# Attention stage of a hybrid decoder trunk: order of the K loads, the class copies, the 1/z chain and the V weights

## The chip, the cores and the metric

The kernel runs on one core of a Trainium2 chip. Its metric is the device time of one launch in microseconds (us), the median of several runs. Beside the times there is one profiled execution, whose trace holds every instruction. The engines are TensorE (PE in the profile; its weight loads are PEld), VectorE (DVE), ScalarE (ACT), GpSimd (POOL) and SyncE (SP). Each takes its instructions in the order in which the program was written for it. SyncE issues most loads, POOL issues the stores and some loads.

## The reference

Two layers over 1024 positions of width 1024, in float32: a gated short convolution with a SwiGLU, then dilated attention with a SwiGLU. The change lies in the attention, whose core is this:

```python
BRANCHES = ((128, 1), (512, 4), (2048, 16))      # window, dilation; 16 heads of 64
qkv = (h @ w_qkv).reshape(bsz, seq, 3, N_HEADS, HEAD_DIM)
for window, dilation in BRANCHES:
    # query t attends to keys t - j*dilation, j = 0..window//dilation
    s = q.k * HEAD_DIM ** -0.5 + rel_bias[t5_bucket(dist)]
    lse = logsumexp(s); o = exp(s - lse) @ v
alpha = softmax(stack(lses))                      # over the three branches
o = sum(alpha * outs)
x = x + o.reshape(bsz, seq, D_MODEL) @ w_out
```

The softmax over branches joins the three to one: the exponentials of all branches share one maximum and one sum z per query and head, and the output is their weighted sum of V times 1/z.

## The kernel before

The program is an order written out by hand: Python generators are stepped in a fixed pattern, and what they emit goes to each engine's queue in that order. Every float32 operand of a large product is split into a high and a low part (`split`, L132): ScalarE rounds (L142), VectorE subtracts (L143), and TensorE makes three products of the parts. Operands live in `PAGES = 41` pages of 128 x 1024 (`page`); a new tile takes a page that an earlier one has left. PSUM has 8 banks, taken in turn.

Weights stand in a list, `raw_src`, in the order of their use. `ensure(upto)` makes all split weights up to an index, and for each it loads raw weights two further (`get_raw`, `load_raw`, L156 on SyncE). `take(key, ahead)` calls `ensure` for the next weight and `ahead` more, and hands the weight out; `op_state[1]` is the index of the next one to be taken. For the V groups a weight is a slab of 128 x 1024, two for each group.

**The attention stage** runs `slot(n)` for n = 0 to 16, called block n here; p, a = divmod(n, 2) is the pair of heads and the head in it. Up to block 13 (`LAG`) a block has two halves of eight steps:

- first half: the scores of head n (`scores`: matmuls L1556 and L1557, additions of the bias on VectorE L1567 to L1607, at the end the maximum over partitions on POOL, L1610), with steps of the dense work in between;
- second half: the values of head n-1 (`values`: L1629, at the end four copies of z and o from PSUM by ScalarE, L1652 and L1653), the softmax of head n at step i = 3 (subtractions L1618, exponentials L1619), the class copies of the next head's K (`classes`, L1540), and more dense work.

The dense work is one generator, `fill()`, 15 steps a block: value groups 1 and 2 (`value_tiles(g, j)`, 40 steps each: j is the half of the positions, b4 one of four tiles of five steps, L1501 to L1503, evicted by ScalarE L1506, stored by POOL L1510), the projections of Q and K for pairs 6 and 7 (36 steps each, `qk.emit` L1129 to L1138), value group 3, and the first half of the output product (`ao`, L370 to L372). Value group 0 runs ahead of block 0. Group 2 (V2 in what follows) starts in block 2, the projections in block 5, group 3 in block 10, the output product in block 12. In block 12 the attended tiles of pairs 0 to 3 are split too.

At the start of a block SyncE gets these loads, in this order: in odd blocks V of the pair (`load_values`, six transfers into `vx`, which has one buffer: they wait for the values of the pair before), then for head n+1 the bias tables (two transfers, L1452 and L1453, two buffers), K (two, L1530 and L1531), Q (two, L1533) and Q's low part (L1534).

**1/z.** In odd blocks `finish(p - 1)` runs for the pair before, in steps: z to DRAM (L1661, POOL) at i = 0 of the first half; z back with 128 partitions (`zc`, L1664, POOL) at i = 3; reciprocal on VectorE (L1666) and its store (`rdram`, L1667, POOL) at i = 0 of the second half; two loads of 1/z spread over 64 partitions each (L1670, POOL) at i = 4. `attended()` then multiplies o by 1/z (L1717, VectorE) and stores it (L1718, POOL), at i = 2 of the second half of the next, even block.

Of the kernel before, what the change touches and what calls it, by code (L numbers as in the profile page):

```python
# [45 lines left out]
SOFT = 4  # L46
FIN0 = 2
AO_WIDE = 5
AO = 4
LAG = 13  # L50
# [48 lines left out]
def trunk(ctx: ExitStack, tc: tile.TileContext, x, gains_in, cwi, ck, cwo, wqkv, wo, relb,  # L99
# [8 lines left out]
    def page(name, dt=F32):  # L108
        return pages.tile([128, 1024], dt, name=name, tag="page", bufs=PAGES)
# [6 lines left out]
    def bank():  # L116
        return psum.tile([128, 512], F32, name="bank", tag="bank")
# [31 lines left out]
    ops, made, op_state = [], {}, [0, 0]  # L149
# [13 lines left out]
    def ensure(upto):  # L163
        while op_state[0] < min(upto + 1, len(ops)):
            key = ops[op_state[0] + 1][0] if op_state[0] + 1 < len(ops) else None
            if key in sums_of:
                sums_of.pop(key)()
            made[op_state[0]] = ops[op_state[0]][1]()
            op_state[0] += 1

    def take(key, ahead=1):
        i = op_state[1]
        assert ops[i][0] == key, (ops[i][0], key)
        ensure(i + ahead)
        op_state[1] += 1
        return made.pop(i)
# [198 lines left out]
    def run(*gens):  # L375
        for _ in zip(*gens):
            pass
        for g in gens:
            for _ in g:
                pass  # L380
# [1068 lines left out]
    def load_bias(h):  # L1449
        t = scope["pool"].tile([128, L1 + L2], F32, name="bias", tag="bias", bufs=2)  # L1450
        base = tables.offset + h * G3
        nc.sync.dma_start(t[:, 0:L1], bass.AP(tensor=tables.tensor, offset=base, ap=[[1, 8], [A1, 16], [1, L1]]))  # L1452
        nc.sync.dma_start(t[:, L1:L1 + L2], bass.AP(tensor=tables.tensor, offset=base + G0,  # L1453
                                                    ap=[[1, 32], [A2, 4], [1, L2]]))
        return t
# [10 lines left out]
    def attention(norm, qk):  # L1466
        KS, KC, QS, wv = {}, {}, {}, []
# [22 lines left out]
        def value_tiles(g, j):  # L1490

            if j == 0:
                wv[:] = [take(("v", g, i), 1) for i in range(2)]
            v = page("v")
            for b4 in range(4):
                t = 4 * j + b4
                b = bank()[:, :256]
                for k in range(KT):
                    (hi, lo), (whi, wlo) = qk.h[j][k], wv[k // 4]
                    a, c = slice(b4 * 128, b4 * 128 + 128), slice(k % 4 * 256, k % 4 * 256 + 256)  # L1500
                    nc.tensor.matmul(b, hi[:, a], whi[:, c], start=k == 0, stop=False)  # L1501
                    nc.tensor.matmul(b, hi[:, a], wlo[:, c], start=False, stop=False)
                    nc.tensor.matmul(b, lo[:, a], whi[:, c], start=False, stop=k == KT - 1)  # L1503
                    if k % 2:
                        yield
                nc.scalar.activation(v[:, b4 * 256:b4 * 256 + 256], b, AF.Identity, scale=norm.r[:, t:t + 1])  # L1506
                yield
            vd = vdram[g]
            for r in range(4):
                nc.gpsimd.dma_start(bass.AP(vd.tensor, vd.offset + (512 * j + r) * 256,  # L1510
                                          [[16 * 256, 32], [4 * 256, 4], [1, 256]]), v[32 * r:32 * r + 32])

        def load_values(p):
            src = vdram[p // 2]
            for a in range(2):
                off = src.offset + p % 2 * 128 + a * 64
                dims = slice(128 * a, 128 * a + 64)
                nc.sync.dma_start(vx[:, 0:8, dims], bass.AP(src.tensor, off, [[256, 128], [128 * 256, 8], [1, 64]]))
                for h in range(2):
                    nc.sync.dma_start(vx[:, 8 + 4 * h:12 + 4 * h, dims],  # L1520
                                        bass.AP(src.tensor, off + 512 * 256 * h, [[1024, 128], [256, 4], [1, 64]]))

        def load_kq(n):

            p, a = divmod(n, 2)
            k, q = qk.kq[p, 1], qk.kq[p, 0]
            rows = lambda t, r: bass.AP(t.tensor, t.offset + r * S, [[S, 64], [1, S]])
            n0, n1 = (slice(64 * i, 64 * i + 64) for i in (a, 1 - a))
            KS[n], QS[n] = page("ka", F32R), page("qa", F32R)
            nc.sync.dma_start(KS[n][n0].bitcast(F32), rows(k, 64 * a))  # L1530
            nc.sync.dma_start(KS[n][n1].bitcast(F32), rows(k, 128 + 64 * a))  # L1531
            for m in (n0, n1):
                nc.sync.dma_start(QS[n][m].bitcast(F32), rows(q, 64 * a))  # L1533
            nc.sync.dma_start(qlo[a][n0].bitcast(F32), rows(q, 128 + 64 * a))  # L1534

        def classes(n):

            KC[n] = page("kca", F32R)
            for h in range(2):
                nc.scalar.activation(KC[n][:, half(h)], view(KS[n], h * HALF, [[1, 4], [4, 128]]), AF.Copy)  # L1540
                yield
# [171 lines left out]
        def attended():  # L1713

            while put_off:
                p, o, z = put_off.pop()
                nc.vector.tensor_tensor(out=o, in0=o, in1=z, op=ALU.mult)  # L1717
                nc.gpsimd.dma_start(odram[p], o)  # L1718

        put_off = []  # L1720
        OZ, acts = {}, {}

        def slot(n, dense, ndense, late=0, hook=iter(())):

            def other(k):
                for _ in range(k):
                    next(dense, None)

            p, a = divmod(n, 2)
            if n < H:  # L1730
                new = dict(bias=bias.pop(n))
                sc = scores(p, a, new)
            else:
                sc = iter(())
            if n <= LAG and n % 2:
                load_values(p)
            if n + 1 < H:
                bias[n + 1] = load_bias(n + 1)
                load_kq(n + 1)
            if n:  # L1740
                q, b = divmod(n - 1, 2)
                if b == 0:
                    OZ[q] = page("o"), page("z")
                old = live.pop(n - 1)
                old.update(o=OZ[q][0], z=OZ[q][1])
                pv = values(q, b, old)
            else:
                pv = iter(())
            extra = later = iter(())
            lagged = n <= LAG  # L1750
            if n + 1 < H:
                later = classes(n + 1)
            if lagged and a and p:
                extra = finish(p - 1)
            used = 0
            if lagged:
                for i in range(8):
                    next(sc, None)
                    if n or i % 2:
                        other(1)  # L1760
                        used += 1
                    if i in (0, 3):
                        next(extra, None)
                run(sc)
            else:
                if a == 0 and not late:
                    other(1)
                    used += 1
                for i in range(8):
                    next(sc, None)  # L1770
                    next(pv, None)
                    next(pv, None)
                    if i >= late and i % 2 == 0:
                        other(1)
                        used += 1
                run(sc)
                run(pv)
                if a == 0:
                    extra = finish(p - 1)
                if a == 0 and n < H:  # L1780
                    load_values(p)
            left = max(ndense - used, 0)
            for i in range(8):
                next(pv, None)
                next(pv, None)
                if i == 2:
                    attended()
                if i in (0, 4) if lagged else i < FIN0 or i > SOFT:
                    next(extra, None)
                if i in (0, 1):  # L1790
                    next(later, None)
                if i == (3 if lagged else SOFT):
                    if n < H:
                        live[n] = new
                        run(softmax(new))
                if i >= SOFT:
                    next(hook, None)
                other(left * (i + 1) // 8 - left * i // 8)
            run(pv)
            run(extra)  # L1800
# [56 lines left out]
        acts.update(split_attended(load_attended(range(AO, 7))))  # L1857
        ensure(ahead_ao)
        slot(H, dense, 15)
        run(dense)  # L1860
        return acts
# [199 lines left out]
```

## Time and profile before

| | us |
|---|---|
| runs: lowest, median, highest of 3 | 2145.25, 2153.15, 2157.45 |
| profiled execution, its own time | 2144.75 |
| its span, first to last instruction | 2142.9 |
| busy in the span: PE, DVE, ACT, POOL | 2109.1, 1747.6, 1008.1, 255.8 |
| mean granted TensorE clock | 0.994 |
| first and last maximum of the attention blocks begin at | 1122.7, 1428.6 |

A row of the timeline is start, duration, engine, line, operation and tiles; what stands in brackets is how long the engine was idle just before, and what ended that. A row of the waits is who waited for whom, the total in us, how often, and the longest. Tiles are named out<-in. Memory transfers are read by the line that issued them.

### The profile page before, as it was taken

To read this page: it belongs to the slowest core of one execution; us is meant where nothing else is said; L and a number is where in the kernel's file an instruction comes from. 1 tells how busy PE (TensorE), PEld (TensorE's weight loads), DVE (VectorE), ACT (ScalarE), POOL (GpSimd) and SP (SyncE) were. 2 spreads that over 40 slices of the span, in tenths; PEclk is the share of its full clock that TensorE was granted. 3 is DMA by queue.
4 is the path that set the end of the run, shared out by engine and by line. 5 is a ranking of instruction groups with operands and counts; after the bars stand their busy time and mean duration, and the time that the engine had idled before them with its cause. 6 is when DMAs were issued, how large, how long until landed. Compare 5 with 4: busy or idle time off the path is not lost. (4 is left out here: it accounts for less than half of the span.)

```text
span 2142.9 us, 30996 instructions
## 1 busy us (share of the span) xinstructions
PE 2109.1 (98%) x11086; PEld 1808.6 (84%) x11086; DVE 1747.6 (82%) x3272; ACT 1008.1 (47%) x1848; POOL 255.8 (12%) x370
## 2 busy tenths in 40 slices
PE   9999999999999999999999999899999999999998
PEld 7788878888888888877898989898788888888887
DVE  8898769988888888868956677787998888888876
ACT  7333426443434464336545545455543434456435
POOL 1000000111101000000322332321010101001000
PEclk9999999999999999999999999999999999999999
DMA  7322642333333576341766777765223333368432
GB/s 218 93 94 69 228 136 69 107 110 104 103 109 112 171 225 195 100 158 41 273 196 168 181 196 191 226 193 163 72 91 101 109 108 106 105 201 236 160 94 79
DMA packets 143353, 304.90 MB, mean 142 GB/s; under 512 B 48942, under 2 KB 55326, under 8 KB 143200
## 3 DMA queue, kind: packets, MB, share of 16 engines
q1 hardware_dynamic: 107488, 201.94, 31.6%
q0 software_dynamic: 28080, 86.29, 12.7%
q10 hardware_dynamic: 7632, 14.70, 1.8%
q8 instruction: 88, 1.44, 0.3%
q14 instruction: 65, 0.53, 0.1%
HBM read 212.48 MB, written 83.05 MB: 138 GB/s over the span
## 5 line engine op out<-in xcount | busy, mean ns | idle before, releaser
L563 PE MATMUL bank<-b,w 128*128 128x512 f32 x1952 | 760.8, 390 | 4.8 <-DVE w L143 4.6
L561 PE MATMUL bank<-b,w 128*128 128x512 f32 x1952 | 762.8, 391 | 2.1 <-ACT w L142 1.7
L562 PE MATMUL bank<-b,w 128*128 128x512 f32 x1952 | 760.4, 390 | 0.6 <-DVE b L872 0.6
L563 PEld LDWEIGHTS bank<-b,w 128*128 128x128 f32 x1952 | 366.4, 188 | 85.6 <-DVE w L143 9.5
L561 PEld LDWEIGHTS bank<-b,w 128*128 128x128 f32 x1952 | 366.7, 188 | 78.6 <-ACT w L142 2.8
L562 PEld LDWEIGHTS bank<-b,w 128*128 128x128 f32 x1952 | 366.7, 188 | 76.5 <-DVE b L872 1.2
L142 ACT ACTIVATE w<-combo 128x512 fp32r<-128x512 f32 (+2 forms) x488 | 249.1, 540 | 231.5 <-DVE combo L190 214.7
L143 DVE TENSOR_TENSOR w<-combo,w 128x512 fp32r<-128x512 f32 (+2 forms) x488 | 277.0, 581 | 37.7 <-ACT w L142 37.0
L567 ACT ACTIVATE part<-bank 128x512 f32<-128x512 f32 x186 | 110.7, 596 | 388.8 <-PE bank L563 387.1
L143 DVE TENSOR_TENSOR w<-raw,w 128x512 fp32r<-128x512 f32 (+2 forms) x342 | 190.0, 577 | 37.2 <-ACT w L142 37.2
L571 DVE TENSOR_TENSOR part<-part,bank 128x256 f32<-128x256 f32 (+1 forms) x366 | 171.1, 498 | 31.1 <-PE bank L563 16.6
L142 ACT ACTIVATE w<-raw 128x512 fp32r<-128x512 f32 (+2 forms) x342 | 166.7, 530 | 45.2 <-PE bank L563 12.2
L370 PE MATMUL bank<-w_hi,w 128*128 128x512 f32 (+1 forms) x400 | 153.3, 383 | 3.3 <-ACT w_hi L142 3.3
L371 PE MATMUL bank<-w_lo,w 128*128 128x512 f32 (+1 forms) x400 | 150.0, 375 | 0.7 <-DVE w_lo L143 0.7
L372 PE MATMUL bank<-w_hi,w 128*128 128x512 f32 (+1 forms) x400 | 149.8, 375 | 0.7 <-DVE w L143 0.7
L791 DVE TENSOR_TENSOR x<-x,bank 128x512 f32<-128x512 f32 x136 | 92.8, 682 | 29.1 <-PE bank L563 29.1
L492 DVE TENSOR_TENSOR x<-x,bank 128x512 f32<-128x512 f32 (+1 forms) x104 | 66.3, 643 | 55.7 <-PE bank L372 55.1
L190 DVE TENSOR_TENSOR combo<-raw 128x512 f32<-128x512 f32 (+1 forms) x172 | 111.4, 648 | 0.0
L370 PEld LDWEIGHTS bank<-w_hi,w 128*128 128x128 f32 x400 | 75.8, 189 | 16.5 <-ACT w_hi L142 3.5
L371 PEld LDWEIGHTS bank<-w_lo,w 128*128 128x128 f32 x400 | 75.8, 190 | 14.4 <-DVE w_lo L143 1.6
L372 PEld LDWEIGHTS bank<-w_hi,w 128*128 128x128 f32 x400 | 75.8, 189 | 14.5 <-DVE w L143 1.1
L554 DVE TENSOR_TENSOR b<-hin,b 128x512 fp32r<-128x512 f32 x126 | 79.6, 686 | 9.5 <-ACT b L553 9.5
(247 smaller groups left out, 3497.6 us busy)
## 6 DMA issues: line engine op xcount, KB each, us to landing
hin<-part SPq DMA_DIRECT2D x126, 256.0 KB
raw<-in_ffn_w_gate SPq DMA_DIRECT2D x44, 512.0 KB
raw<-in_ffn_w_up SPq DMA_DIRECT2D x44, 512.0 KB
part<-sum POOLq DMA_DIRECT2D x72, 256.0 KB, 2.3
raw<-in_ffn_w_down SPq DMA_DIRECT2D x48, 384.0 KB
raw<-in_attn_w_qkv SPq DMA_DIRECT2D x27, 512.0 KB
raw<-in_conv_w_in SPq DMA_DIRECT2D x24, 512.0 KB
part<-part POOLq DMA_DIRECT2D x36, 256.0 KB, 2.4
```

Of the source, the lines that this page charges most:

```text
L142: nc.scalar.activation(hi, src, AF.Copy)
L143: eng.tensor_tensor(out=lo, in0=src, in1=hi, op=ALU.subtract)
L190: eng.tensor_tensor(out=c, in0=a, in1=b, op=op)
L370: nc.tensor.matmul(b, whi[:, a], ahi[:, s], start=first, stop=False)
L371: nc.tensor.matmul(b, whi[:, a], alo[:, s], start=False, stop=False)
L372: nc.tensor.matmul(b, wlo[:, a], ahi[:, s], start=False, stop=last)
L561: nc.tensor.matmul(b, hi[:, a], bhi, start=start and k == 0, stop=False, skip_group_check=True)
L562: nc.tensor.matmul(b, hi[:, a], blo, start=False, stop=False, skip_group_check=True)
L563: nc.tensor.matmul(b, lo[:, a], bhi, start=False, stop=k == n - 1, skip_group_check=True)
L567: nc.scalar.activation(t, b, AF.Copy)
L571: nc.vector.tensor_tensor(out=t, in0=t, in1=b, op=ALU.add)
L791: nc.vector.tensor_tensor(out=X[n][:, half(h)], in0=X[n][:, half(h)], in1=b, op=ALU.add)
```

## The change

- In `value_tiles` the two slabs of a group are taken without asking for the next weight. In the second half of a group (j = 1), ahead of its second and third tile, the next weight and the one after it are asked for.
- In a block's loads K of the next head comes first. The V loads of an odd block come right behind that K, ahead of Q; the bias tables come last.
- The class copies are made at i = 1 and 2 of the second half instead of 0 and 1.
- `finish` of a pair: the z store and load stay; the reciprocal and its store move from i = 0 to i = 6 of the odd block's second half, the loads of the spread 1/z from i = 4 there to i = 2 of the next block's first half. `attended()` moves from i = 2 to i = 5 of the second half in blocks up to 14.

```diff
@@ value_tiles
             if j == 0:
-                wv[:] = [take(("v", g, i), 1) for i in range(2)]
+                wv[:] = [take(("v", g, i), 0) for i in range(2)]
             v = page("v")
             for b4 in range(4):
+                if j and b4 in (1, 2):
+                    ensure(op_state[1] + b4 - 1)
@@ load_kq
             nc.sync.dma_start(KS[n][n1].bitcast(F32), rows(k, 128 + 64 * a))
+            if n <= LAG + 1 and n % 2 == 0 and n:
+                load_values(p - 1)
             for m in (n0, n1):
@@ slot
-        put_off = []
+        put_off, ending = [], []
...
-            if n <= LAG and n % 2:
-                load_values(p)
             if n + 1 < H:
+                load_kq(n + 1)
                 bias[n + 1] = load_bias(n + 1)
-                load_kq(n + 1)
...
             if lagged and a and p:
-                extra = finish(p - 1)
+                ending.append(finish(p - 1))
...
-                    if i in (0, 3):
-                        next(extra, None)
+                    if a and ending and i in (0, 3):
+                        next(ending[-1])
+                    if a == 0 and ending and i == 2:
+                        run(ending.pop())
...
+                    if ending and i == 2:
+                        run(ending.pop())
...
-                if i == 2:
+                if i == (2 if n > LAG + 1 else 5):
                     attended()
-                if i in (0, 4) if lagged else i < FIN0 or i > SOFT:
+                if lagged and a and ending and i == 6:
+                    next(ending[-1])
+                if not lagged and (i < FIN0 or i > SOFT):
                     next(extra, None)
-                if i in (0, 1):
+                if i in (1, 2):
                     next(later, None)
```

## The prediction

> **What bounds the kernel now.** I read the page's first two lines, then the stretches (busy time and granted clock piece by piece) over the attention stage, which the diff edits, then TensorE's timeline there for its idle time.
>
> ```profile
> span 2142.9 us, 30996 instructions
> PE 2109.1 (98%) x11086; PEld 1808.6 (84%) x11086; DVE 1747.6 (82%) x3272; ACT 1008.1 (47%) x1848; POOL 255.8 (12%) x370
> ```
> ```profile
> 1110.00:1440.00 330.00, 314.43 (x2290) 294.74 (x2289) 241.66 (x431) 160.21 (x228) 100.10 (x102) 0.97 0.73 192
> 1150.00:1160.00 10.00, 9.89 (x87) 9.70 (x85) 6.52 (x12) 3.45 (x5) 5.25 (x5) 1.00 0.73 191
> 1160.00:1170.00 10.00, 5.90 (x29) 5.61 (x30) 4.22 (x7) 6.99 (x11) 0.56 (x1) 0.66 0.15 41
> 1270.00:1280.00 10.00, 9.07 (x49) 7.97 (x50) 9.90 (x22) 4.29 (x6) 2.15 (x5) 0.83 0.38 121
> 1350.00:1360.00 10.00, 8.88 (x74) 8.74 (x75) 9.11 (x18) 6.17 (x11) 3.35 (x3) 1.00 0.63 201
> 1360.00:1370.00 10.00, 6.27 (x40) 5.39 (x39) 7.70 (x10) 7.61 (x11) 3.66 (x6) 0.85 0.44 154
> 1370.00:1380.00 10.00, 9.72 (x50) 8.30 (x49) 6.54 (x13) 3.61 (x6) 1.14 (x2) 0.81 0.75 170
> ```
> ```profile
> 1130.78 0.36 PE L1556 MATMUL bank<-qa,ka 128*128 128x256 f32 x1 [0.89 <-DVE lf L1567]
> 1163.42 0.58 PE L1501 MATMUL bank<-w_hi,b 128*128 128x256 f32 x1 [3.54 <-ACT w_hi L142]
> 1270.44 0.38 PE L1556 MATMUL bank<-qa,ka 128*128 128x256 f32 x1 [1.28 <-ACT o L1653]
> 1271.67 0.79 PE L370 MATMUL bank<-b,w_hi 128*128 128x512 f32 x1 [0.48 <-ACT o L1653]
> 1312.23 0.38 PE L1556 MATMUL bank<-qa,ka 128*128 128x256 f32 x1 [1.15 <-ACT o L1653]
> 1350.95 0.38 PE L1556 MATMUL bank<-qa,ka 128*128 128x256 f32 x1 [2.36 <-ACT v L1506]
> 1366.93 0.79 PE L370 MATMUL bank<-w_hi,w 128*128 128x512 f32 x1 [3.26 <-ACT w_hi L142]
> 1368.19 0.80 PE L371 MATMUL bank<-w_lo,w 128*128 128x512 f32 x1 [0.47 <-DVE w_lo L143]
> ```
>
> TensorE is 98% busy: 33.8 us of idle in the whole span, 15.6 of it between 1110 and 1440. So only two things can be won: its idle time, and the low clock behind some of it. In a stretch the columns are its length, the busy time and count of PE, PEld, DVE, ACT and POOL, the granted clock, the DMA's share and rate. Four places carry nearly all of the loss. **V2** (start of value group 2, in block 2): 29 matmuls from 1160 to 1170 against 87 just before, so 10 x (1 - 29/87) = 6.7 us. **End of block 7** (1270): 1.28 + 0.48 idle, and a clock of 0.83, which costs 1.7 of 10 us: together 3.5. **End of block 11** (1351): 2.36 at full clock. **Start of the output product** in block 12 (1367): 3.26 + 0.47, and 1.5 + 1.9 of clock, together 7.1. Smaller: 0.89 at the start of block 1, 1.15 at the end of block 9. In all 21.7 us, 1.0% of the kernel: the most that edits in this stage can bring.
>
> **Weights asked for inside the V group.**
>
> ```profile
> 1161.40 1.02 ACT L1619 ACTIVATE lp<-lp 128x384 f32<-128x384 f32 x2
> 1162.33 1.99 ACT L142 ACTIVATE w_hi<-raw 128x1024 fp32r<-128x1024 f32 x2
> 1164.34 0.59 ACT L1652 ACTIVATE z<-bank 64x512 f32<-64x512 f32 x1
> 1168.90 0.31 PE L1556 MATMUL bank<-qa,kca 128*128 128x256 f32 x1
> 1113.82 2.27 DVE w_lo L143 x2
> ```
>
> The second slab of V2 is split only when its group begins, behind head 2's exponentials on ScalarE; TensorE needs it after a few matmuls and stands until 1163.42. After the change both slabs of a group are split while the group before is in its second half: V2's behind block 1's softmax and at the start of block 2, 15 and 10 dense steps ahead. Number and size of splits and slab loads stay the same. The wait goes whole unless something else is late there. Next in line are the exponentials, done at 1162.42, while TensorE would be back at the scores at 1168.90 - 6.7 = 1162.2; the z and o copies that free banks follow at 0.6 us each, and TensorE has banks for its first scores without them. I take 6.7, with 4.3 as the lower bound (a wait for four copies, 2.4) and 6.7 as the upper.
>
> The same edit takes V1's two splits (2.27 us at 1113.82 in the chain of waits) out from between head 0's scores on VectorE and puts them ahead of block 0, where VectorE idles. The 0.89 us at 1130.78 is a wait for score additions that these held up: I take 0.9, bounds 0 and 0.9. On SyncE two slab loads now stand ahead of head 1's K; its use is put a step later as well, and costs nothing while the matmuls of V0 and V1 cover it; -1.0 if not (two issues, and their bytes ahead of K's).
>
> At the output product the wait is for the split of an attended tile, which stays where it is. One split of `ao` moves away from there, and the multiply of o by 1/z moves to just behind the first split. Both lie beside TensorE's value matmuls: 0, bounds -1.2 (one multiply) and +0.7 (one half-wide split).
>
> **1/z half a block later.**
>
> ```profile
> DVE zc L1666 <- DMA zc<-zdram: 24.4, 4, 9.0
> ACT kca L1540 <- DMA ka<-kq: 28.0, 8, 10.8
> SPq L1518 <- PE bank L1629: 68.3, 8, 16.6
> ```
> ```profile
> 1257.25 3.18 POOL L1610 PARTITION_ALL_REDUCE mb<-m  x1
> 1263.63 0.25 DVE L1666 RECIPROCAL zc<-zc 128x16 f32<-128x16 f32 x1 [8.23 <-DMA zc<-zdram]
> 1291.98 2.36 DVE L143 TENSOR_TENSOR w_lo<-raw,w_hi 128x1024 fp32r<-128x1024 f32 x2 [3.54 <-ACT w_hi L142]
> 1335.71 0.69 DVE L1607 TENSOR_TENSOR m<-m,lp 128x512 f32<-128x512 f32 x1
> 1340.14 3.18 POOL L1610 PARTITION_ALL_REDUCE mb<-m  x1
> 1345.45 0.25 DVE L1666 RECIPROCAL zc<-zc 128x16 f32<-128x16 f32 x1 [9.05 <-DMA zc<-zdram]
> ```
>
> The reciprocal stands ahead of the softmax on VectorE. In block 7 the maximum is ready at 1260.43, but VectorE waits for `zc` until 1263.63: everything behind it (exponentials, z and o copies, the bank that TensorE waits for at 1270) is 3.2 us late. In block 11 it is 1345.45 - 1343.32 = 2.1. Placed behind the softmax, some 4 us later, the reciprocal finds `zc` landed. Block 7 gains its 3.5, since the delay removed is above the 1.76 idle (bounds 1.8, the idle alone, and 3.5); block 11 gains 2.1 (bounds 0, if VectorE is late by itself, and 2.4). Elsewhere `zc` cost TensorE nothing.
>
> What is added: the write of 1/z and the two loads of its spread move with it. The loads now stand on POOL in an even block, ahead of that head's maximum.
>
> ```profile
> 1197.52 1.22 DVE L1717 TENSOR_TENSOR o<-o,z 128x1024 f32<-128x1024 f32 x1
> 1197.86 3.96 POOL L1610 PARTITION_ALL_REDUCE mb<-m  x1 [4.97 <-issue]
> 1302.84 3.22 POOL L1610 PARTITION_ALL_REDUCE mb<-m  x1 [2.96 <-DVE m L1607]
> 1305.92 0.56 POOL L1667 DMA_DIRECT2D rdram<-zc  x1
> 1308.97 1.15 DVE L1618 TENSOR_TENSOR lp<-lp,mb 128x384 f32<-128x384 f32 x2
> 1313.33 1.04 POOL L1670 DMA_DIRECT2D z<-rdram  x2 [5.78 <-DMA rdram<-zc]
> 1320.45 4.06 POOL L1610 PARTITION_ALL_REDUCE mb<-m  x1 [4.96 <-DVE m L1607]
> ```
>
> From block 9 to 10: the softmax's last subtraction ends at 1310.12, the reciprocal takes 0.25, the write goes out at 1310.6. It took 1313.33 - 1305.92 = 7.4 until the loads went, so they go at 1318.0 and end at 1319.0; head 10's maximum began at 1320.45: 1.4 us spare. The stores of the projections' K and Q that share POOL are held in another half of the block, as long as now, and are read blocks later; so is the store of o. The multiply (1.22) leaves the maximum's window, where the maximum took 3.96 and 4.06 instead of 3.22, and comes behind the softmax: 0.7 to 0.8 earlier for the exponentials, 0.4 to 0.5 later for VectorE's next scores. Behind block 8 that hides in VectorE's 3.54 us wait ahead of 1291.98, behind block 10 in POOL's lateness (VectorE ready at 1336.40, maximum begun at 1340.14). Block 9's 1.15 falls by 0.6 or so through the shorter maximum before it. I take +0.6, bounds -1.5 (0.5 late in three blocks) and +1.2.
>
> **K first, copies a step later.**
>
> ```profile
> 1377.71 0.53 SPq L1530 DMA_DIRECT2D ka<-kq  x1
> 1384.79 2.17 ACT L1540 ACTIVATE kca<-ka 128x512 fp32r<-128x512 f32 x2 [10.82 <-DMA ka<-kq]
> ```
>
> In odd blocks SyncE waits at the loads of V for TensorE's last values, up to 16.6 us at a time, and the next head's K stands behind that: ScalarE waits 10.82 us for the K issued at 1377.71. The change issues K ahead of that wait. Q and the bias tables come up to six issues of 0.53 later, 3.2 us, in a block of 17.6 (1302.84 to 1320.45), and are first read in the next block. The two copies of 1.1 us stay ahead of the softmax on ScalarE, which waits for the maximum there. ScalarE's 28.0 us mostly go, but TensorE has no idle row behind them; the dense product covers them. 0, bounds 0 and +1; without that cover the 10.82 would show.
>
> **Sum.** 6.7 + 0.9 + 3.5 + 2.1 + 0.6 = 13.8 us off; bounds 4.3 + 0 - 1.0 - 1.2 + 1.8 + 0 - 1.5 = 2.4 and 6.7 + 0.9 + 0.7 + 3.5 + 2.4 + 1.2 + 1 = 16.4. The profiled execution took 2144.75 us (1.85 around its span), so it would take 2131. The three runs have a median of 2153.15, 8.4 above it; I carry the sum to that: 2153.15 - 13.8 = 2139.
>
> After 1.28 + 0.48 us of idle the clock was 0.83 in 1270 to 1280; after 2.36 at 1351 it was 1.00 in 1350 to 1360. The Trainium skill (TensorE: Matmul & The Clock Gate, section Why this matters for your kernels) says that only idle gaps over about 3 us drop the clock. By that rule block 7's share is 1.8 and the sum 12.1; the row at 1270 speaks against it, so the trace's 3.5 stands.
>
> **The rivals.** *The waits are handed on.* VectorE was busy 9.90 of 10 us from 1270 on. If its own work, not the landing of `zc`, holds the blocks with projections, blocks 7, 9 and 11 stay as they are and only V2 and block 1 gain: 7.6 off, 2145.5. For it: that row. Against: 8.23 and 9.05 us of pure waiting just ahead of the two stalls. *Slower: the spread loads hold the maximum.* POOL works in order; from 7.4 + 1.4 = 8.8 us for a 1/z write on, each even head's maximum starts late, in six blocks (4 to 14). At 2 us late each, with 3.4 us of low clock behind each gap as after 1367, that is 6 x 5.4 = 32 us more against 13.8: 2171. Against: at 1302.84 and 1320.45 POOL waited for VectorE, not the other way. *It does nothing:* a slab could be late from memory instead of from ScalarE; but slabs are loaded a group ahead. 2153.
>
> **How the numbers follow.** About 0.5% (10.8 us) is what a measurement of this kernel can tell from no change. Forecast 0.57, over that; handed on 0.29 and nothing 0.04, within it; spread loads 0.10, slower. The forecast's own range is 2142 (10.8 off the median) down to 2128 (16.4 off the profiled execution, if runs like it become the rule); handed on and nothing reach 2153. So 2128 to 2154.
>
> **What would show it.** Right: no idle at the first use of V2's slabs; VectorE's wait for `zc` under 4 us; ScalarE's wait for `ka` under 8; one place of low clock left in the stage (the output product); TensorE's idle time between 1110 and 1440 down from 15.6 to about 6. Wrong: a maximum that begins over 1 us after VectorE's last `m`, with a load of z from `rdram` just ahead on POOL; idle at the ends of blocks 7 and 11 as before; SyncE held at a page ahead of a K load.

## The result, and the profile after

| | us |
|---|---|
| before, 7 runs on one chip: lowest, median, highest | 2145.25, 2150.91, 2157.45 |
| after, 7 runs: lowest, median, highest | 2136.76, 2139.53, 2143.59 |
| after / before | 0.995, 95% interval 0.9933 to 0.9968 |
| after, profiled execution, its own time | 2143.59 |
| whole change once more, 5 runs beside 21 of before | 2140.21 against 2149.14: 0.9956 (0.9944 to 0.9969) |

The change takes 10.8 us off by the first ratio (0.005 x 2150.91) and 9.5 by the second (0.0044 x 2149.14). The forecast of 2139.0 lies 0.5 from the median. Part of that nearness is luck: the three runs that the forecast started from had a median of 2153.15, 1 to 4 us above what later sets of runs gave, and the sum of 13.8 was 3 to 4 us too large.

The two profiled executions hide the gain. That of before (2144.75) lies below the lowest of its seven runs, that of after (2143.59) was the highest of its own. So the profile of the second measurement of the whole change (2136.84) is read beside it. The stage itself runs from the first matmul of value group 0 to the first of the SwiGLU; the timeline of TensorE has both ends, for before, after, and the change once more:

```profile
1088.68 0.28 PE L1501 MATMUL bank<-w_hi,b 128*128 128x256 f32 x1
1496.92 0.39 PE L561 MATMUL bank<-b,w 128*128 128x512 f32 x1
```
```profile
1092.50 0.28 PE L1503 MATMUL bank<-w_hi,b 128*128 128x256 f32 x1
1495.55 0.39 PE L561 MATMUL bank<-b,w 128*128 128x512 f32 x1
```
```profile
1091.04 0.28 PE L1503 MATMUL bank<-w_hi,b 128*128 128x256 f32 x1
1489.01 0.39 PE L561 MATMUL bank<-b,w 128*128 128x512 f32 x1
```

408.2 us before, 403.1 after, 398.0 the second time. In both profiles of the change the stage begins 2.4 to 3.8 us later than in before's, and that is why the first two spans differ by only 1.4. The change doesn't make this: in the kernel with the multiply alone (below), whose code up to there is before's, the stage begins at 1092.12, and in the kernel with both of the next weights at one place, whose code up to there is after's, at 1088.42.

The stretches of after, as shown for before (length, then busy time and count of PE, PEld, DVE, ACT and POOL, granted clock, DMA share and rate), with one stretch more, 1410 to 1420; then the row of the whole stretch in the change's second profile:

```profile
1110.00:1440.00 330.00, 315.58 (x2332) 297.39 (x2331) 239.91 (x432) 163.49 (x234) 98.52 (x102) 0.98 0.72 197
1160.00:1170.00 10.00, 9.97 (x86) 9.76 (x84) 6.46 (x12) 3.62 (x6) 5.25 (x5) 1.00 0.46 129
1270.00:1280.00 10.00, 10.00 (x71) 9.16 (x70) 6.51 (x14) 2.71 (x3) 5.39 (x5) 1.00 0.42 134
1360.00:1370.00 10.00, 7.41 (x27) 5.73 (x28) 6.52 (x7) 9.11 (x13) 3.31 (x6) 0.68 0.35 109
1410.00:1420.00 10.00, 7.49 (x50) 6.88 (x49) 3.49 (x9) 0.00 (x0) 2.62 (x5) 0.88 0.50 179
```
```profile
1110.00:1440.00 330.00, 319.13 (x2356) 300.41 (x2355) 245.76 (x441) 166.39 (x239) 99.05 (x103) 0.99 0.73 201
```

V2's hole (5.90 busy, 29 matmuls, clock 0.66 in 1160 to 1170) is filled: 9.97 and 86. The stretch from 1270, 0.83 before, is at full clock and full load. But idle time between 1110 and 1440 did not fall from 15.6 to 6: it is 14.4 in after (330 - 315.58) and 10.9 in the second profile. TensorE's gaps in after show where it went; the second fence is the change's second profile. A gap that waits for copies of o is named after the block that makes these copies at its end; it stands among the first scores of the next block.

```profile
1171.20 0.38 PE L1560 MATMUL bank<-qa,ka 128*128 128x256 f32 x1 [1.23 <-ACT o L1657]
1172.43 0.38 PE L1560 MATMUL bank<-qa,ka 128*128 128x256 f32 x1 [0.49 <-ACT o L1657]
1247.66 0.38 PE L1560 MATMUL bank<-qa,ka 128*128 128x256 f32 x1 [1.15 <-ACT o L1657]
1308.62 0.38 PE L1560 MATMUL bank<-qa,ka 128*128 128x256 f32 x1 [1.60 <-ACT o L1657]
1361.34 0.80 PE L370 MATMUL bank<-w_hi,w 128*128 128x512 f32 x1 [4.92 <-ACT w_hi L142]
1417.37 0.39 PE L1560 MATMUL bank<-qa,ka 128*128 128x256 f32 x1 [2.51 <-DVE x L492]
```
```profile
1169.76 0.38 PE L1560 MATMUL bank<-qa,ka 128*128 128x256 f32 x1 [1.26 <-ACT o L1657]
1305.77 0.38 PE L1560 MATMUL bank<-qa,ka 128*128 128x256 f32 x1 [1.14 <-ACT o L1657]
1358.15 0.80 PE L370 MATMUL bank<-w_hi,w 128*128 128x512 f32 x1 [4.59 <-ACT w_hi L142]
```

No gap is left at V2's first use, at the start of block 1, or at the ends of blocks 7 and 11. New are a gap at the end of block 2 (1.23 + 0.49), one at the end of block 6 (1.15, and 0.56 in the second profile), a longer one at the output product (4.92 and 4.59, was 3.26), and in after alone one in block 15 (2.51). That at the end of block 9 stays (1.60 and 1.14, was 1.15). Who waited between 1110 and 1440, by total, times and longest, in after:

```profile
POOL zc L1668 <- DMA zdram<-z: 28.3, 6, 5.7
DVE w_lo L143 <- ACT w_hi L142: 21.0, 8, 7.7
DVE zc L1670 <- DMA zc<-zdram: 7.3, 1, 7.3
```

VectorE's wait for `zc` fell from 24.4 us in four to 7.3 in one, and ScalarE's 28.0 for `ka` is gone from the list. VectorE's wait for a split by ScalarE, on the other hand, grew from 11.0 in five to 21.0 in eight.

### The profile page after: what moved, and what is told of

The parts are those of the page before. It is cut to its first block, busy times and chain, and to the rows that moved or that the text cites. A ratio compares the mean times of both kernels' runs of the same rounds, so it can differ in the third digit from the quotient of the medians.

```text
span 2141.5 us, 31004 instructions
## 1 busy us (share of the span) xinstructions
PE 2108.1 (98%) x11086; PEld 1807.9 (84%) x11086; DVE 1744.0 (81%) x3272; ACT 1007.4 (47%) x1848; POOL 254.2 (12%) x370
## 3 DMA queue, kind: packets, MB, share of 16 engines
q0 software_dynamic: 28080, 86.29, 12.7%
## 4 chain that ended last, share of the span: by engine, by line
PE 82%; DVE 7%; issue 3%; ACT 2%; DMA 2%; POOL 1%; SPq 0%; DVEq 0%; POOLq 0%; ACTq 0%
PE bank L563 19%; PE bank L561 19%; PE bank L562 19%; PE bank L371 4%; PE bank L372 4%; PE bank L370 4%; PE bank L653 3%; PE bank L656 3%; PE bank L655 3%; PE bank L1633 2%; POOL mb L1614 1%; PE bank L1503 1%; PE bank L1504 1%; PE bank L1505 1%; DVE w L143 1%
```

## The experiments

Medians and ratios stand against before's runs on the same chip; us off are worked out from ratio and before's median. First the three parts, each alone on the kernel before, beside the whole.

**The weights alone** (the `value_tiles` hunk).

```diff
-                wv[:] = [take(("v", g, i), 1) for i in range(2)]
+                wv[:] = [take(("v", g, i), 0) for i in range(2)]
+                if j and b4 in (1, 2):
+                    ensure(op_state[1] + b4 - 1)
```

> The kernel before with the weights edit alone. Sum of the prediction: 6.7 us at V2 and 0.9 at block 1, so 7.6 us off (ratio 0.9965), no idle of TensorE and no low clock at the start of V2. Rival (handed on inside the block): the two splits now stand between head 2's score additions on VectorE, so that the maximum of head 2 starts late; then TensorE idles at the end of block 2 for a bank and only 4 to 5 us come off (0.998). The waits at the ends of blocks 7 and 11 stay by both.

Measured: 2144.29 (11 runs) against 2149.14 (21), 0.9979 (0.997 to 0.9988): 4.5 off. TensorE's gaps:

```profile
1167.96 0.38 PE L1558 MATMUL bank<-qa,ka 128*128 128x256 f32 x1 [1.26 <-ACT o L1655]
1345.82 0.58 PE L1558 MATMUL bank<-qa,ka 128*128 128x256 f32 x1 [2.15 <-ACT v L1508]
1365.62 0.79 PE L370 MATMUL bank<-w_hi,w 128*128 128x512 f32 x1 [6.27 <-ACT w_hi L142]
```

V2's stall is gone. From the first score of one block to that of the next, block 2 falls from 25.2 to 18.4 us, the 6.7 of the forecast, and block 1 from 19.6 to 18.3. But block 3 rises from 18.4 to 20.6: some of it is handed on, as the rival said, and the 4.5 is its 4 to 5. VectorE's timeline in block 2 shows how (here from the change's second profile, where it is the same):

```profile
1147.92 1.23 DVE L143 TENSOR_TENSOR w_lo<-raw,w_hi 128x1024 fp32r<-128x1024 f32 x1 [1.94 <-ACT w_hi L142]
1149.06 0.75 DVE L1571 TENSOR_TENSOR lf<-bank,bias 128x256 f32<-128x256 f32 x2
1151.67 1.23 DVE L143 TENSOR_TENSOR w_lo<-raw,w_hi 128x1024 fp32r<-128x1024 f32 x1 [1.86 <-ACT w_hi L142]
```

Both of V2's subtractions now stand among head 2's score additions, and VectorE waits for ScalarE's rounding ahead of each: 1.94 + 1.86 idle and 2 x 1.23 of work. Its last maximum `m` of head 2 then comes 7.8 us after the last score instead of 3.0, and everything behind that (exponentials, copies of o, the bank of the next scores) is late. The gap at the output product grows too, from 3.26 to 6.27. Of the gaps at the ends of blocks 7 and 11, which were to stay, the second did; for the first there is one of 2.27 at the end of block 6.

**1/z alone** (all hunks with `ending`, and `attended()` at i = 5).

```diff
-                extra = finish(p - 1)
+                ending.append(finish(p - 1))
...
+                    if a == 0 and ending and i == 2:
+                        run(ending.pop())
...
-                if i == 2:
+                if i == (2 if n > LAG + 1 else 5):
                     attended()
...
+                if lagged and a and ending and i == 6:
+                    next(ending[-1])
```

> The kernel before with the move of the reciprocal, of the spread loads and of the multiply alone. Sum of the prediction: 3.5 + 2.1 + 0.6 = 6.2 us off (ratio 0.9971); VectorE's wait for zc falls from 24.4 us to under 8, no idle at the ends of blocks 7 and 11, V2's stall of 6.7 us as before. Rival (VectorE's own work holds the blocks): the wait for zc goes but the idle at the ends of blocks 7, 9 and 11 stays, 0 to 2 us off (0.999 to 1.000). Second rival (the spread loads hold the maximum): maxima of even heads start late, slower.

Measured: 2139.44 (5 runs), 0.9954 (0.9941 to 0.9966): 9.9 off, as much as the whole change. Its gaps are before's without those at the ends of blocks 7 and 11:

```profile
1163.73 0.58 PE L1501 MATMUL bank<-w_hi,b 128*128 128x256 f32 x1 [3.54 <-ACT w_hi L142]
1308.35 0.39 PE L1556 MATMUL bank<-qa,ka 128*128 128x256 f32 x1 [1.06 <-ACT o L1653]
1359.76 0.49 PE L370 MATMUL bank<-w_hi,w 128*128 128x512 f32 x1 [3.23 <-ACT w_hi L142]
```

**The loads and class copies alone** (the `load_kq` hunk, K ahead of V and the bias tables, copies at i = 1 and 2).

```diff
-            if n <= LAG and n % 2:
-                load_values(p)
             if n + 1 < H:
+                load_kq(n + 1)
                 bias[n + 1] = load_bias(n + 1)
-                load_kq(n + 1)
...
-                if i in (0, 1):
+                if i in (1, 2):
                     next(later, None)
```

> The kernel before with the order of the loads (K, V, Q, bias) and the class copies a step later, and nothing else. Sum of the prediction: 0 (ratio 1.000, within 1 us), ScalarE's wait for ka falls from 28 us to under 8. Rival (late K is what makes the kernel before vary from run to run): 3 us or more off (0.9985 or less), and the spread of its times is narrower than that of before.

Measured: 2149.79 (11 runs), 1.0001 (0.9992 to 1.001): nothing, to about 2 us. ScalarE's wait for `ka` cost nothing, and taking it away gained nothing.

**The whole change again**, on the chip of the three parts.

> The whole change again, for a second profile and its ratio beside its parts. If the parts add up, its gain is the sum of those of the weights, the 1/z move and the loads alone (13.8 us by the prediction, 11.4 measured); if they share a wait, less than the sum; if one part clears the way for another, more. The idle that its first profile had in block 15 (2.51 us) and at the ends of blocks 2, 6 and 9 comes again if it is made by the order of the work, and not if it came from a late transfer in that one execution.

Measured: 2140.21 (5 runs), 0.9956 (0.9944 to 0.9969): 9.5 off. The parts add up to 4.5 + 9.9 - 0.2 = 14.2, 4.7 more than the whole. That is no more than the noise can make: the four intervals reach 1.9, 2.7, 1.9 and 2.7 us to each side, and the root of the sum of their squares is 4.7. So a loss between the parts is possible, but not shown. The gap at the end of block 2 came again, those at the ends of blocks 6 and 9 smaller, that in block 15 not.

**The change without its weights edit** (the two `value_tiles` lines as before).

> The whole change without its weights edit: 1/z move, loads and class copies. The 1/z move alone took 9.7 us off, the whole 8.9 beside it. Theory (the weights edit's 4.8 us are lost again elsewhere when the 1/z move is there): the same time as the whole change within 1.5 us, with V2's stall of 6.7 us as in the kernel before, and shorter waits elsewhere: at the start of the output product (under 4 us against 4.6 and 4.9) and none at the ends of blocks 2 and 6. Rival (the loads edit costs something beside the 1/z move, which hides the weights' gain): slower than the whole change by 3 us or more.

Measured: 2142.45 (5 runs) against 2151.94 (9), 0.9961 (0.9948 to 0.9973): 8.4 off. The whole had 9.5 and 10.8, with intervals of over 2 us to each side. So beside the 1/z move the weights edit is worth 1 to 2 us by these ratios, and 4.5 (2.6 to 6.4) alone; the noise doesn't tell the two apart. What it does at its own place can be read. From the first score of block 1 to that of block 6, for 1/z alone and for the change's second profile:

```profile
1124.36 0.29 PE L1556 MATMUL bank<-qa,kca 128*128 128x256 f32 x1
1224.98 0.28 PE L1556 MATMUL bank<-qa,kca 128*128 128x256 f32 x1
```
```profile
1126.43 0.29 PE L1560 MATMUL bank<-qa,kca 128*128 128x256 f32 x1
1221.01 0.28 PE L1560 MATMUL bank<-qa,kca 128*128 128x256 f32 x1
```

100.6 us without the weights edit, 94.6 with it; with the old 1/z chain, 100.4 in before and 94.9 in the weights alone. In these blocks the edit gains 5.5 to 6.0 either way, and the 1/z move takes nothing of that. It loses some behind them. After V3 the next weights are those of the output product, and in block 12 their halves are now split among head 12's score additions (the change's second profile, VectorE):

```profile
1339.64 0.69 DVE L143 TENSOR_TENSOR w<-raw,w 128x512 fp32r<-128x512 f32 x1 [1.87 <-ACT w L142]
1343.01 0.68 DVE L143 TENSOR_TENSOR w<-raw,w 128x512 fp32r<-128x512 f32 x1
```

That is 1.87 of waiting and 1.37 of work ahead of the softmax that the first output product waits for. With the 1/z move the gap there is 3.20 to 3.23 us in the two kernels without the weights edit, and 4.55 to 4.92 in three profiles with it (3.57 in the next experiment, where these halves are split earlier). With the old chain it is 3.18 to 4.04 in three kernels without the edit, and 6.27 with it. So the edit costs 1.3 to 1.7 us there beside the 1/z move and 2.2 to 3.1 alone: this is a part of what it loses against the forecast, but not a loss that comes from the two together.

**Both of the next weights at one place.**

```diff
-                if j and b4 in (1, 2):
-                    ensure(op_state[1] + b4 - 1)
+                if j and b4 == 1:
+                    ensure(op_state[1] + 1)
```

> The changed kernel, with both next weights asked for at the second tile of the half (after block 1's softmax for V2) instead of one there and one at the third tile. Theory (the split at the start of block 2 blocks VectorE among head 2's score additions for 1.9 + 1.2 us, and so makes the 1.2 + 0.5 us of idle at the end of block 2): that idle is gone, 1.5 to 2 us faster. Rival (VectorE has to do the same work anyway before head 2's maximum): the idle stays, within 1 us of the change.

Measured: 2139.15 (5 runs), 0.9941 (0.9928 to 0.9953): 12.7 off. VectorE now waits for ScalarE once in block 2, for both subtractions:

```profile
1145.30 2.36 DVE L143 TENSOR_TENSOR w_lo<-raw,w_hi 128x1024 fp32r<-128x1024 f32 x2 [1.94 <-ACT w_hi L142]
```

Head 2's `m` comes 4.9 us after the last score, not 7.8, and the gap of 1.26 + 0.49 is gone. The step that handed the stall on is shown. But the edit hands it on again: gaps of 0.48 at the end of block 1 and of 0.52 + 0.51 at the end of block 4 are new, and the last also stands in the kernel below that has this edit among others (0.51 + 0.49). From the first score of block 1 to that of block 6 this kernel takes 95.4 us, not 94.6. So by these profiles the 2 to 3 us in the total, which lie within the intervals, were not won here.

**Pair 6's reciprocal later**, in block 15's first half; the store and load of z stay in block 14. In block 14 and on there is no lag, and the change leaves pair 6's chain as it was. In after VectorE stood for its `zc`:

```profile
1416.51 0.25 DVE L1670 RECIPROCAL zc<-zc 128x16 f32<-128x16 f32 x1 [7.30 <-DMA zc<-zdram]
```

```diff
+                    if n == H - 1 and i == 1:
+                        next(ending[-1])
+                    if n == H - 1 and i == 5:
+                        run(ending.pop())
...
```

> The changed kernel, with pair 6 treated like the others: z is stored and loaded in block 14 as now, the reciprocal and its store move to i = 1 of block 15's first half, the spread loads to i = 5 there. Theory (the whole change loses about 4 us in most runs to VectorE's wait for zc of pair 6, seen in its first profile as 7.3 us of VectorE, 2.51 of TensorE and 1.7 of clock): 3 us or more faster than the change, about 2136.5, and no idle in block 15. Rival (that wait was one execution's late transfer): the same time as the change within 1 us.

Measured: 2138.31 (5 runs), 0.9944 (0.993 to 0.9957): 12.1 off, 1 to 3 more than the change, within the intervals. The gap in block 15 is not there, but neither is it in the change's second profile. So it is a gap of some executions, and how often it comes was not settled.

**The attended tiles' splits ahead of the softmax** in block 12.

```diff
-                if i >= SOFT:
+                if i >= (0 if lagged else SOFT) and i != 3:
                     next(hook, None)
```

> The changed kernel, with the four attended tiles split at i = 0, 1, 2 and 4 of block 12's second half, ahead of its softmax but for the last, instead of i = 4 to 7. The wait at the start of the output product is 4.6 + 0.5 + 0.5 us of idle and up to 3.4 of clock in the change's profiles. Theory (the splits wait behind the exponentials, as V2's did): 6 to 9 us faster than the change, 2131 to 2134. Rival (a tile comes late from memory, or VectorE's part of the splits delays the softmax by as much): under 2 us.

Measured: 2135.94 (5 runs), 0.9933 (0.992 to 0.9946): 14.4 off, 3.6 to 4.9 more than the change, between the theory and the rival; the intervals overlap. The gap at the output product falls to 1.82 us:

```profile
1308.99 0.38 PE L1560 MATMUL bank<-qa,ka 128*128 128x256 f32 x1 [3.73 <-ACT o L1657]
1363.62 0.50 PE L370 MATMUL bank<-w_hi,w 128*128 128x512 f32 x1 [1.82 <-ACT w_hi L142]
```

Some is given back: block 12 takes 18.3 instead of 26.5 us, block 13 25.2 instead of 20.9. Three of the four subtractions now run beside the maximum. They take 5.18 us together, end 0.9 after it, and it took 4.04 instead of 3.22. The first row is a loss that came in this execution, 3.73 us at the end of block 9, and POOL's timeline has its cause:

```profile
1290.61 0.56 POOL L1665 DMA_DIRECT2D zdram<-z  x1
1299.04 0.57 POOL L1668 DMA_DIRECT2D zc<-zdram  x1 [7.87 <-DMA zdram<-z]
1299.64 3.18 POOL L1614 PARTITION_ALL_REDUCE mb<-m  x1
```

The load of `zc` stands ahead of head 9's maximum on POOL and waits for the store of z to land. Here it held POOL until 1299.04, and the maximum began 2.8 us after VectorE's last `m`. In the kernel without the weights edit and in that with both at one place it was 2.4, with gaps of 3.28 and 3.27 us.

**The load of `zc` behind the maximum.**

```diff
-                    if a and ending and i in (0, 3):
+                    if a and ending and i == 0:
                         next(ending[-1])
...
-                if lagged and a and ending and i == 6:
+                if lagged and a and ending and i in (0, 6):
                     next(ending[-1])
```

> The change, with the load of z into zc moved from i = 3 of the odd block's first half to i = 0 of its second half, so that on POOL it stands behind that head's maximum instead of ahead of it. Theory (this load, which waits for the store of z to land, is what holds head 9's maximum): head 9's maximum begins within 0.5 us of VectorE's last m, no gap over 1.5 us at the end of block 9, and 1 to 2 us below the change. Rival (the maximum is late for another reason, or the late load now makes the reciprocal wait for zc): maximum as late as before, or VectorE waiting over 2 us for zc in blocks 3 to 13; same time as the change or up to 3 us above it.

Measured: 2137.8 (6 runs) against 2149.36 (23), 0.9948 (0.9933 to 0.9963): 11.2 off, where the change had 9.5 and 10.8. Head 9's maximum begins 0.1 us after `m`, as expected, but the reciprocal is late instead:

```profile
1340.79 0.25 DVE L1670 RECIPROCAL zc<-zc 128x16 f32<-128x16 f32 x1 [3.64 <-DMA zc<-zdram]
1358.70 0.80 PE L370 MATMUL bank<-w_hi,w 128*128 128x512 f32 x1 [7.52 <-ACT w_hi L142]
```

Both theories were right at one place each. The wait of 3.64 us stands ahead of head 12's score additions, and 7.52 us of idle follow at the output product.

**The multiply alone, and the chain alone.** The 1/z move has two halves: `attended()` from i = 2 to i = 5, and the chain of reciprocal, store and spread loads.

```diff
-                if i == 2:
+                if i == (2 if n > LAG + 1 else 5):
                     attended()
```

> Before, with the multiply of o by 1/z alone moved from i = 2 to i = 5 of an even block's second half (behind the softmax); reciprocal, store and spread loads of 1/z stay where they were. Theory (the reciprocal ahead of the softmax costs the time, the multiply next to nothing): within 1.5 us of the kernel before, idle at the ends of blocks 7 and 11 as before. Rival (the multiply beside the maximum carries what the 1/z move gained above the 6.2 us that were forecast): 3 to 4 us below the kernel before, through a maximum of 3.2 instead of 4.0 us in six blocks.

Measured: 2147.39 (12 runs), 0.9997 (0.9986 to 1.0007): 0.6 off, and no more than 3. The other half leaves the multiply at i = 2 and moves the chain:

> Before, with the reciprocal, its store and the spread loads of 1/z moved as in the change, but the multiply left at i = 2. Theory: nearly all of what both moves gained together (9.7 us), so 8 to 10 us below the kernel before, and no idle at the ends of blocks 7 and 11. Rival (multiply carries the part above the forecast): 6 us below. A third case: the multiply at i = 2 now waits for spread loads that went out half a block later, and blocks the softmax: slower than the kernel before.

Measured: 2145.07 (12 runs), 0.9978 (0.9969 to 0.9988): 4.7 off, half of the 9.9. The theory named the wrong amount. The rival's 6 lies within the interval, but not its reason, since the multiply alone gained nothing. The third case had the mechanism, at one place, though not the sign of the total:

```profile
1359.50 1.23 DVE L1717 TENSOR_TENSOR o<-o,z 128x1024 f32<-128x1024 f32 x1 [6.55 <-DMA z<-rdram]
1366.62 0.80 PE L370 MATMUL bank<-w_hi,w 128*128 128x512 f32 x1 [7.41 <-ACT w_hi L142]
```

The gaps at the ends of blocks 7 and 11 are gone. But in block 12 the multiply, ahead of the softmax, stands 6.55 us for the spread loads that go out half a block later, 3.1 of them after the maximum was ready at 1356.44, and the gap at the output product is 7.41 instead of 3.23. The two halves are one edit: whoever makes a result later must move its reader too.

**Four edits more on the change**: the two splits at one place, pair 6, the attended tiles' splits, `zc` behind the maximum.

> The change with four edits more: zc loaded behind the maximum, pair 6's reciprocal and spread loads in block 15's first half, the attended tiles' splits at i = 0, 1, 2 and 4 of block 12, both next V weights asked for at the second tile. If their gains were independent (the three that were tried alone gained 1 to 4 us each): 5 to 7 us below the change, 15 to 18 below the kernel before. Rival (they share one cover, as the weights edit and the 1/z move did): no lower than the best of them alone, 13 to 15 below the kernel before.

Measured: 2132.09 (6 runs), 0.9922 (0.9907 to 0.9937): 16.8 off, the fastest of all, and 6 to 7 us below the change by the ratios. That is the first case, though the interval (13.5 to 20.0 off) reaches into the rival's 13 to 15. What is left:

```profile
1302.33 0.38 PE L1560 MATMUL bank<-qa,ka 128*128 128x256 f32 x1 [1.05 <-ACT o L1657]
1358.52 0.80 PE L370 MATMUL bank<-w_hi,w 128*128 128x512 f32 x1 [4.57 <-ACT w_hi L142]
```
```profile
1339.64 0.25 DVE L1670 RECIPROCAL zc<-zc 128x16 f32<-128x16 f32 x1 [2.93 <-DMA zc<-zdram]
1347.44 5.19 DVE L143 TENSOR_TENSOR w_lo<-oin,w_hi 128x1024 fp32r<-128x1024 f32 x3
```

The second fence is VectorE's: the wait for `zc` ahead of head 12's score additions, as in the kernel with the late load alone, and the three early subtractions, just behind head 12's last `m`. The gap at the output product is 4.57, where the splits alone left 1.82; the 2.93 us of waiting are about the difference. So two of the edits seem to meet here; that was not tested.

## Why the prediction was right, and where its steps were off

**The total** came out within 0.5 us, by a base that was too high and a sum that was too large.

**Weights: 7.6 forecast (V2 6.7, block 1 0.9), 4.5 measured alone, 1 to 2 beside the rest by ratios that can't tell these apart.** The stall went whole, as the step said, and block 1 gave 1.3. What it named as late next, exponentials and the copies that free banks, was the right place. TensorE had banks for its first scores without them, but not for those behind, and stood 1.26 + 0.49 us. The step's lower bound of 4.3 allowed for such a wait, its value of 6.7 did not. It priced the order on ScalarE and left out that the subtractions on VectorE would stand among head 2's additions and wait there. That is 2.2 us in block 3. The step also priced the split of `ao` that leaves the output product (0, bound 0.7), but not that the split lands ahead of head 12's maximum: 1.3 to 3.1 us more idle there instead of 0. Together these are as large as the 3.1 that the weights alone fell short.

**1/z: 6.2 forecast (3.5, 2.1 and 0.6), 9.9 measured.** The mechanism held: no idle at the ends of blocks 7 and 11, and VectorE's 24.4 us for `zc` gone but for pair 6. Between the two profiles the stage is 7.7 shorter (408.2 and 400.6): block 8, with the gap at the end of block 7, by 4.1 us (3.5 forecast), and block 12, with that at the end of block 11 and the output product, by 3.4 (2.1 forecast). For the rest up to 9.9 the base matters: the profiled execution was faster than all of before's seven runs. Other profiles with the old chain lose more at single places: the kernel with the multiply alone has 2.31 us of idle at the end of block 9 (1.15 in the profiled one), that with the loads alone 2.47 and a clock of one half for 3.4 us behind it. By the whole stage only the second is longer than before's (413.5; the first 407.7). Whether such losses make up the rest was not measured. The 0.6 for a shorter maximum at block 9 did not come (the gap is still 1.14 to 1.60), and could not: the maximum just ahead of this gap, head 9's, took 3.22 us before already, and the multiply stands in even blocks only.

**Loads and class copies: 0 forecast, 0 measured.** 28.0 us of waiting that nobody behind it needed.

**The rivals.** *Handed on* named the wrong owner: the blocks with projections did gain. But the thing itself happened in block 2. *Spread loads hold the maximum* is refuted for what it named: with these loads ahead, every even head's maximum begins 0.2 us after `m`. What can hold a maximum is the neighbour on the same queue, the load of `zc`, in odd blocks; before had that too (3.7 us in block 11).

**The signs that were to show it.** V2 and `ka` came as named. Of VectorE's wait for `zc` one of 7.3 us is left, over the 4 named (4.4 in the second profile): it is pair 6's, whose chain the change leaves as it was. "One place of low clock" came in the change's second profile, but for two in after. Idle of "about 6" failed: 10.9 and 14.4, by the gaps at the ends of blocks 2, 6 and 9, the longer one at the output product, and block 15 in after.

## What to carry to other kernels

A wait that is removed is paid out only as far as the step that moved finds an engine with time to spare: price the moved instruction on every engine that it uses, and look at what stands right behind it there. A chain of small transfers and its reader move together, or the reader becomes the new wait. And take the size of a stall from more than one execution if it hangs on the landing of a transfer: here the one that was profiled was faster than all seven runs. Before a loss is put down to two edits together, see whether each has it alone.

## What the runs showed of the hardware

A small transfer takes long. The stores of z, 8 KB each, from issue to landing (last line of that line's view in after):

```profile
DMA to landing us min/median/max: 2.8/5.9/6.3
```

The reciprocal needs such a store and then a load, one behind the other, and the readers of 1/z another pair.

The same idle gap was followed by a lower clock in one execution and not in another. At the end of block 2, 1.24 + 0.51 us of idle in the kernel with early splits, and 1.26 + 0.49 in the change's second profile, gave these stretches:

```profile
1169.00:1179.00 10.00, 9.33 (x65) 9.13 (x66) 5.58 (x13) 4.68 (x8) 4.34 (x3) 0.83 0.68 165
```
```profile
1169.00:1179.00 10.00, 8.75 (x73) 8.54 (x74) 6.46 (x15) 5.25 (x9) 4.37 (x3) 1.00 0.78 188
```

0.83 and 1.00. Single gaps do the same: 2.36 us at the end of block 11 left a clock of 1.00 in before, 2.37 at the end of block 6 were followed by 0.83 (1246 to 1256) in the kernel with pair 6's reciprocal later. The Trainium skill (TensorE: Matmul & The Clock Gate, section Why this matters for your kernels) puts the limit at gaps of about 3 us. The first of the two rows doesn't agree: the clock fell with idle of 1.75 in all. A gap below 3 us may cost clock, then, and the forecast was right to count block 7's; what decides it within 1 to 2.5 us, these runs don't show.

A maximum over partitions on POOL and VectorE's multiply cost each other time, and the one that began second paid. In before the multiply began first beside heads 4, 8, 10 and 15: the maximum took 3.75 to 4.06 us, the multiply 1.22. Beside heads 12 and 14 the maximum began first: it took 3.22, and the multiply 2.50 and 2.63. Moving the multiply away gained nothing that could be measured by itself.
